# Seven half-size products per pair of columns in the up-projection of a ConvFFN

## The chip, the cores and the metric

One core of one Trainium2 chip runs the kernel. The metric is the device time of one execution in microseconds (us). The kernel before takes 2165.48 us, the median of 3 runs from 2164.55 to 2167.25.

## The reference

The layer mixes tokens in three ways (RWKV-7, latent attention, differential attention), gates and sums the three, projects with w_o and adds the input. Then comes the part that the change is in:

```python
h = RMSNorm(x)                                   # 1024 tokens x 1024
u = h @ w_up                                     # 1024 x 5632: 2816 gate, 2816 val
up = jnp.pad(u, ((0, 0), (CONV_WIDTH - 1, 0), (0, 0)))
u = sum(conv_w[j] * up[:, j:j + S] for j in range(CONV_WIDTH)) + conv_b   # causal, width 3
gate, val = jnp.split(u, 2, axis=-1)
x = x + (jax.nn.silu(gate) * val) @ w_down       # then a final RMSNorm
```

All of it is float32.

## The kernel before, in words

A float32 matmul is made of three: each operand is split into a high part (rounded to the matmul's format) and a low part (the rest), and hi*hi, hi*lo and lo*hi are summed in PSUM. `hilo` makes the parts: ACT copies the high part, POOL or DVE subtracts it for the low part.

`phase_o` takes 8 blocks of 128 tokens: two times 24 matmuls with w_o, DVE adds x out of PSUM, ACT squares and sums, DVE and POOL make the inverse root (`rs_v`, `rs_r`), DVE multiplies (`y`), TensorE transposes y (`ntp`), ACT and DVE write its parts `h2h`, `h2l` (model dimension on the partitions, 8 chunks k of 128; 1024 tokens in the free dimension).

`phase_up` takes the 5632 columns in 44 blocks of 128, gate j and val j alternating (j = 0 to 21). For each block it loads 512 KB of weights, makes their parts (`whi` on ACT, `wlo` on POOL) and runs 2 token halves x 8 chunks x 3 = 48 matmuls of 128x512 into one of two PSUM tiles `ups`. The convolution reads PSUM: ACT writes tap 2 and the bias into SBUF (`cv`), DVE adds the two other taps. ACT takes Silu of the gate, POOL multiplies it with val, and the product `g` stays in SBUF.

`phase_down` does two token groups of 512. In each it goes over 22 blocks j: weights `wdr` from DRAM into parts `wdh`, `wdl` (ACT, DVE), g's parts `gh`, `gl`, and 24 matmuls into 8 accumulators `dps`, one PSUM bank each.

A list scheduler sets the order of each engine's instructions from program order and dependences; every engine then works through its queue in order. All loads and stores here are issued by SP's queue, in order as well. The helpers record the operations, so that in the profile nearly all matmuls are line 65, DVE's and POOL's `tensor_tensor` line 89, `scalar_tensor_tensor` line 99, and ACT's line 86.

## Time and profile before

| | |
|---|---|
| median of 3 runs | 2165.48 us (2164.55 to 2167.25) |
| the profiled execution | 2172.32 us, of which the span is 2170.5 us |
| PE busy | 2098.8 us, 97% |
| DVE, ACT, POOL busy | 945.1, 740.2, 694.0 us |
| output projection | about 1343 to 1438 us |
| up-projection | about 1438 to 1922 us |
| down-projection | about 1913 to 2170 us |
| mean granted clock of TensorE | 0.989 of full speed |

PE, DVE, ACT and POOL are TensorE, VectorE, ScalarE and GpSimd. In a timeline row stand the start, the duration, the engine, the line, the operation, output and inputs with partitions x elements, and in brackets how long the engine was idle before and what released it. A row with "x2" merges two instructions that follow each other; its duration is that of both.

### The profile page before, as it was taken

What the parts mean: (1) busy time and instruction counts of PE and PEld (TensorE: products, weight loads), DVE (VectorE), ACT (ScalarE), POOL (GpSimd) and SP (SyncE); (2) the same over time, 40 slices, a digit from 0 to 9 for tenths busy, and PEclk for the clock granted to TensorE, in tenths of its full rate; (3) what the DMA queues carried; (4) which work ended last, traced back from release to release, by engine and by line L of the source; (5) the groups of instructions that cost most, each with busy time, mean ns of one, the idle gap of its engine ahead of it and who ended that gap; (6) DMA issues with size and microseconds to landing.
All of it is one profiled execution on the core that took longest, in us unless ns stands there. A gap on an engine that the chain in (4) does not pass through costs nothing. (4 is left out here: it accounts for less than half of the span.)

```text
span 2170.5 us, 32037 instructions
## 1 busy us (share of the span) xinstructions
PE 2098.8 (97%) x12818; PEld 1680.4 (77%) x12818; DVE 945.1 (44%) x1956; ACT 740.2 (34%) x1270; POOL 694.0 (32%) x522
## 2 busy tenths in 40 slices
PE   7999999999999998999888999999999999999998
PEld 6877777777777776777677777888888888878887
DVE  7035255243433523566677764432222222243534
ACT  5332222232232223666545442232222222232322
POOL 3152333152243323364155556013333333300000
PEclk9999999999999999999999999999999999999999
DMA  5222232122222214300375444221111111142521
GB/s 178 84 71 78 63 88 66 51 85 62 73 68 78 82 60 131 95 16 11 94 221 175 149 145 160 97 80 49 49 49 49 49 49 49 39 155 98 174 98 59
DMA packets 127447, 191.39 MB, mean 88 GB/s; under 512 B 60064, under 2 KB 64032, under 8 KB 127296
## 3 DMA queue, kind: packets, MB, share of 16 engines
q1 hardware_dynamic: 127296, 189.32, 27.3%
q8 instruction: 101, 1.65, 0.3%
q14 instruction: 50, 0.41, 0.1%
HBM read 147.32 MB, written 41.96 MB: 87 GB/s over the span
## 5 line engine op out<-in xcount | busy, mean ns | idle before, releaser
L89 POOL TENSOR_TENSOR wlo<-wraw,whi 128x512 fp32r<-128x512 f32 (+1 forms) x174 | 276.1, 1594 | 582.4 <-ACT whi L86 245.3
L65 PE MATMUL gps<-hhi,whi 128*128 128x512 f32 (+1 forms) x880 | 346.5, 397 | 8.1 <-ACT sp L86 5.4
L65 PE MATMUL gps<-hlo,whi 128*128 128x512 f32 (+1 forms) x880 | 342.6, 392 | 0.0
L86 ACT ACTIVATE whi<-wraw 128x512 fp32r<-128x512 f32 (+1 forms) x174 | 128.0, 737 | 426.4 <-DMA wraw<-in_w_rest_dram 106.3
L65 PE MATMUL gps<-hhi,wlo 128*128 128x512 f32 (+1 forms) x880 | 226.2, 394 | 2.1 <-DVE lx L99 1.7
L65 PEld LDWEIGHTS gps<-hhi,whi 128*128 128x128 f32 x880 | 168.0, 191 | 49.4 <-ACT sp L86 6.2
L65 PEld LDWEIGHTS gps<-hlo,whi 128*128 128x128 f32 x880 | 167.9, 191 | 36.0 <-issue 4.5
L65 PEld LDWEIGHTS gps<-hhi,wlo 128*128 128x128 f32 x880 | 157.4, 188 | 43.1 <-issue 6.7
L89 POOL TENSOR_TENSOR rs_r<-rs_v,phalf 128x1 f32<-128x1 f32 (+2 forms) x43 | 40.2, 935 | 391.9 <-DVE rs_v L96 383.8
L86 ACT ACTIVATE L<-L,m 128x128 f32<-128x128 f32 (+7 forms) x128 | 98.8, 772 | 69.1 <-DVE m L89 47.5
L77 PE MATMUL ptp<-ident,L 128*128 128x128 f32 x432 | 72.4, 282 | 10.7 <-DVE L L99 2.9
L89 DVE TENSOR_TENSOR gl<-g,gh 128x512 fp32r<-128x512 f32 x43 | 29.5, 692 | 108.8 <-ACT gh L86 107.6
L99 DVE SCALAR_TENSOR_TENSOR st<-pr,gam,fc 128x64 f32<-128x64 f32 x60 | 17.0, 283 | 128.0 <-PE pr L65 127.8
L86 ACT ACTIVATE gh<-g 128x512 fp32r<-128x512 f32 x43 | 26.8, 630 | 131.9 <-PE dps__19477 L65 67.2
L77 PEld LDWEIGHTS ptp<-ident,L 128*128 128x128 f32 x432 | 49.2, 142 | 26.9 <-issue 15.0
L89 POOL TENSOR_TENSOR g<-cv 128x1024 f32<-128x1024 f32 x22 | 52.6, 2390 | 51.7 <-DVE cv L99 50.2
L878 DVE CUSTOM_DVE_ANT_0 L<-S,mband,rq 128x512 f32<-128x512 f32 (+3 forms) x96 | 57.1, 612 | 19.5 <-PE ptp L77 9.7
L89 DVE TENSOR_TENSOR wdl<-wdr,wdh 128x1024 fp32r<-128x1024 f32 x44 | 53.8, 1225 | 15.9 <-ACT wdh L86 15.9
L86 ACT ACTIVATE sp<-gps,hbg 128x512 f32<-128x512 f32 x48 | 32.9, 686 | 75.1 <-PE gps L65 67.9
L65 PE MATMUL bps<-oh,whi 128*128 128x512 f32 x128 | 53.2, 421 | 5.1 <-DVE merged L99 3.2
L89 POOL TENSOR_TENSOR merged<-merged,gth 128x512 f32<-128x512 f32 x32 | 47.6, 1491 | 29.1 <-DVE gth L99 26.3
L878 DVE CUSTOM_DVE_ANT_0 L<-S,bias 128x512 f32<-128x512 f32 (+3 forms) x96 | 50.7, 551 | 12.5 <-PE ptp L77 6.1
(998 smaller groups left out, 4824.3 us busy)
## 6 DMA issues: line engine op xcount, KB each, us to landing
wraw<-in_w_up_dram SPq DMA_DIRECT2D x44, 512.0 KB, 3.3
wdr<-in_w_down_dram SPq DMA_DIRECT2D x44, 512.0 KB, 3.3
wraw<-in_w_rest_dram SPq DMA_DIRECT2D x80, 256.0 KB, 2.9
pD<-sp SPq DMA_DIRECT2D x78, 256.0 KB, 2.0
gth<-pD SPq DMA_DIRECT2D x48, 256.0 KB, 3.0
x<-in_x_dram SPq DMA_DIRECT2D x16, 512.0 KB, 5.5
wraw<-in_w_rw_dram SPq DMA_DIRECT2D x28, 256.0 KB, 3.0
draw<-pD SPq DMA_DIRECT2D x24, 256.0 KB, 5.0
```

Of the source, the lines that this page charges most:

```text
L65: ins = self.nc.tensor.matmul(out, lhsT, rhs, start=start, stop=stop)
L77: self.marked(self.nc.tensor.transpose(out, in_, ident))
L86: self.nc.scalar.activation(out, in_, func, **kw)
L89: (eng or self.nc.vector).tensor_tensor(out, a, b, op)
L99: self.nc.vector.scalar_tensor_tensor(out, a, s, b, op0, op1)
L878: self.nc.vector.tensor_tensor_reduce(L[:, c0:c0 + w], ps[:, :w], bias[:, c0:c0 + w], scale, 3.0e38, ALU.add, ALU.min, acc)
```

## The change

The up-projection of a pair (gate j, val j) is a product of a 2 x 2 block matrix (token halves by halves of the model dimension) with a 2 x 2 block matrix (halves of the model dimension by gate and val). It is now formed by seven products of half the model dimension (12 matmuls each) instead of eight, in the order n2, m4, m3, n5, m1, m6, m7. Each has an operand that is a sum or difference of halves of h, and a weight that is a sum or difference of halves of the two weight blocks:

- The operands of h (`xn2h`, `xm4h`, ... and their low parts) are made in `phase_o` by `operands`, block by block, instead of `h2h` and `h2l`. The halves of blocks 0 to 3 are kept in DRAM (`hD`) and loaded again with blocks 4 to 7; the operands of m6 and m7 go through DRAM as well.
- Per pair DVE makes five weight sums (`wsum`); ACT makes the seven high parts, DVE three low parts (n2, m1, m7) and POOL four. They are made about a pair ahead.
- n2, m3 and m6 are accumulated in PSUM bank b, m4, n5 and m7 in bank c, m1 in bank a. What stands in a bank after each product is read out by ACT (n2, m1) or DVE (the others) into `C` tiles of gate and val, with the sums that the seven products need.
- The convolution reads the `C` tiles. ACT writes tap 2 and bias into a PSUM tile `cvp`, DVE adds the second tap in place there, and the third into SBUF (`cv`). There is one `cvp` tile.
- The product g is stored to DRAM (`gD`) and loaded again by `phase_down` (`down_g`). The weights and g of the first two down blocks are loaded and split during the last pairs, and `down_first` runs their 48 matmuls first.
- From the last block of `phase_o` to the end of `phase_up`, the matmuls are pinned to program order. The products n2 and m4 of pair 0 stand ahead of the last block's transposes.
- Earlier phases: the tiles `merged`, `d0` and `raw` are allocated in token halves, and one load is made in two.

```diff
-    def mm(self, out, lhsT, rhs, start=True, stop=True):
-        ins = self.nc.tensor.matmul(out, lhsT, rhs, start=start, stop=stop)
+    def mm(self, out, lhsT, rhs, start=True, stop=True, **k):
+        ins = self.nc.tensor.matmul(out, lhsT, rhs, start=start, stop=stop, **k)
+        if self.pinned:
+            self.tc.keep_in_program_order(ins)
...
+                if b == 7:
+                    ts = rows()
+                    for m, k in (("n2", 0), ("m4", 4)):
+                        self.up_w[0, m] = self.up_weight(0, m, [t[:, k:k + 4] for t in ts])
+                    self.pinned = True
+                    for m in ("n2", "m4"):
+                        self.up_begin(0, m)
+                    wo.close()
+                    self.up_open(up)
+                    for m in ("n2", "m4"):
+                        self.up_prepare(1, m)
+                y, p = self.norm_rows(x, g, o2, 1), []
...
+    def operands(self, b, p, sp):
...
+        (h0, l0), (h1, l1) = ([t[:, :, bs] for t in self.X[n]] for n in names)
+        self.act(neg, first, scale=-1.0)
+        self.tt(dif, second, neg, ALU.add)
+        self.act(h0, first, scale=-1.0)
+        self.stt(l0, first, -1.0, f32v(h0), ALU.mult, ALU.subtract)
+        self.hilo(h1, l1, dif, lo_eng=vec)
...
+        self.tt(a, a, neg, ALU.add, pool)
+        d = T("xd") if b < 7 else dif
+        self.tt(d, dif, a, ALU.subtract)
+        self.nc.sync.dma_start(kept[2], d)
+        self.tt(c, c, neg, ALU.subtract, pool)
+        self.nc.sync.dma_start(kept[3], c)
+        h, l3, l1 = self.m1(bs)
+        self.act(h, a, scale=-1.0)
+        self.stt(l3, a[:, 0:3], -1.0, f32v(h[:, 0:3]), ALU.mult, ALU.subtract)
+        self.stt(l1, a[:, 3:4], -1.0, f32v(h[:, 3:4]), ALU.mult, ALU.subtract)
...
+            x, y, op = {"n2": ((1, 0), (1, 1), ALU.add), "m4": ((1, 1), None, None), "m3": ((0, 0), None, None),
+                        "n5": ((0, 0), (0, 1), ALU.add), "m1": ((0, 0), (1, 1), ALU.add),
+                        "m6": ((1, 0), (0, 0), ALU.subtract), "m7": ((0, 1), (1, 1), ALU.subtract)}[n]
...
+        vec = w or n in ("n2", "m1", "m7") or j == NFF
...
+        terms = [(k, a, c) for k in range(4) for a, c in ((0, 0), (0, 1))] + [(k, 1, 0) for k in range(4)]
+        for i, (k, a, c) in enumerate(terms):
+            self.mm(ps, w[a][:, k], col(x[c], k), first and i == 0, i == 11, skip_group_check=not first)
...
+            def after(j, n, ps):
+                u, (gate, val) = self.pairs[j], C[j % 2]
+                if n in ("n2", "m1"):
+                    u[n] = T(n)
+                    self.act(u[n], ps)
+                elif n == "m4":
+                    self.tt(val[:, lo], ps, u["n2"], ALU.subtract)
+                elif n == "m3":
+                    u["w"] = T("w")
+                    self.tt(u["w"], ps, val[:, lo], ALU.add)
+                elif n == "n5":
+                    self.stt(gate[:, hi], ps, -1.0, u["w"], ALU.mult, ALU.add)
+                elif n == "m6":
+                    self.tt(val[:, hi], ps, u["m1"], ALU.add)
+                elif n == "m7":
+                    self.tt(gate[:, lo], ps, u["m1"], ALU.add)
+                    conv(j)
...
+                for e in (1, 0):
+                    c, t = j + NFF * e, T("cv%d" % e, S)
+                    x = C[j % 2][e]
+                    ps = cvp.tile([128, S], F32, tag="cv", name="cvp")
+                    self.act(ps, x[:, 2:S + 2], AF.Identity, scale=cw[:, c, 2:3], bias=cw[:, c, 3:4])
+                    self.stt(ps, x[:, 1:S + 1], cw[:, c, 1:2], ps, ALU.mult, ALU.add)
+                    self.stt(t, x[:, 0:S], cw[:, c, 0:1], ps, ALU.mult, ALU.add)
                     ts.append(t)
-                self.act(ts[0], ts[0], AF.Silu)
-                self.tt(self.g[:, j], ts[0], ts[1], ALU.mult, nc.gpsimd)
+                self.act(ts[1], ts[1], AF.Silu)
+                self.tt(ts[1], ts[1], ts[0], ALU.mult, nc.gpsimd)
+                nc.sync.dma_start(self.gD[j], ts[1])
...
+            for j in range(2, NFF):
+                for n in self.ORDER:
+                    after(j, n, self.up_begin(j, n))
+                    self.up_prepare(last[0] + 1, last[1])
+                    last = j, n
+                    if n == "n5":
+                        loads(j + 2)
```

Three places show how the instructions now stand. The first is DVE's queue in the steady up-projection. Before, it held only the two steps of each column's convolution and, once, a low part for the down-projection (`g`):

```order
L99 SCALAR_TENSOR_TENSOR cv<-ups__15996,cw,cv 128x1023 [waits DMAHW0_49,Activation_49]
L99 SCALAR_TENSOR_TENSOR cv<-ups__15996,cw,cv 128x1022 [waits DVE_49]
L99 SCALAR_TENSOR_TENSOR cv<-ups__16055,cw,cv 128x1023 [waits Activation_49]
L99 SCALAR_TENSOR_TENSOR cv<-ups__16055,cw,cv 128x1022 [waits DVE_49]
L89 TENSOR_TENSOR g_18636<-g,g_18636 128x512 [waits DMAHW7_49,Activation_49]
```

Now, from the reading of m6 to that of the next pair's m4 (`C_16166` and `C_16165` are val and gate of one pair, `C_16164` val of the next; `m_` and `n_` are the copies of m1 and n2):

```order
L102 TENSOR_TENSOR C_16166<-ups_b,m_17855 128x512 [waits PE_49,Activation_49]
L102 TENSOR_TENSOR wsum_16087<-wraw 128x512 [waits DMAHW0_49,Pool_49]
L112 SCALAR_TENSOR_TENSOR cvp<-C_16166,cw,cvp 128x1024 [waits Activation_49]
L102 TENSOR_TENSOR C_16165<-ups_c,m_17855 128x512 [waits PE_49]
L102 TENSOR_TENSOR wl<-wsum,wh 128x512 [waits Activation_49]
L112 SCALAR_TENSOR_TENSOR cv_17893<-C_16166,cw,cvp 128x1024 [waits DVE_49]
L102 TENSOR_TENSOR wsum<-wraw 128x512 [waits DVE_49]
L102 TENSOR_TENSOR wl<-wsum_16086,wh 128x512 [waits PE_49,Activation_49]
L102 TENSOR_TENSOR wsum_16086<-wraw 128x512 [waits DVE_49]
L112 SCALAR_TENSOR_TENSOR cvp<-C_16165,cw,cvp 128x1024 [waits Activation_49]
L102 TENSOR_TENSOR C_16164<-ups_c,n_17925 128x512 [waits PE_49]
```

The reading of m4 stands as the eleventh row, ten behind the reading of m6: behind three convolution steps, three sums and two low parts; the fourth step follows it.

The second is DVE's queue at the last block of the output projection. Before, from the block's first addition of x to the low parts of its transposes:

```order
L89 TENSOR_TENSOR x_15880<-ops__15882,x_15880 128x512 [waits DMAHW5_49,DMAHW4_49,PE_49]
L89 TENSOR_TENSOR h2l<-ntp,h2h 128x4x128 [waits Activation_49] x2
L89 TENSOR_TENSOR x_15880<-ops__15908,x_15880 128x512 [waits PE_49]
L96 TENSOR_SCALAR rs_v<-ss 128x1 [waits Activation_49]
L99 SCALAR_TENSOR_TENSOR y<-x_15880,rs_r,gain 128x1024 [waits Pool_49]
L89 TENSOR_TENSOR h2l<-ntp,h2h 128x4x128 [waits Activation_49] x2
```

Now, what stands between the second addition of x and the same block's y (`dif`, `xn5l`, `xm1a`, `xm1b`, `xm3l` and `xd` belong to the block before it, the `wsum` and `wl` to pairs 0 and 1):

```order
L102 TENSOR_TENSOR wsum_16086<-wraw 128x512 [waits DMAHW5_49]
L102 TENSOR_TENSOR wsum_16087<-wraw 128x512
L102 TENSOR_TENSOR dif<-ntp,neg 128x512 [waits Activation_49]
L112 SCALAR_TENSOR_TENSOR xn5l<-ntp,xn5h 128x4x128 [waits Activation_49]
L102 TENSOR_TENSOR wl<-wsum,wh 128x512 [waits DVE_49,Activation_49]
L109 TENSOR_SCALAR rs_v<-ss 128x1 [waits Activation_49]
L102 TENSOR_TENSOR wsum<-wraw 128x512 [waits DMAHW2_49,DVE_49]
L112 SCALAR_TENSOR_TENSOR xm1a<-xa,xm1b 128x3x128 [waits Activation_49]
L112 SCALAR_TENSOR_TENSOR xm1b<-xa,xm1b 128x128
L102 TENSOR_TENSOR wl<-wsum_16087,wh 128x512 [waits Activation_49]
L102 TENSOR_TENSOR xm3l<-dif,xm3h 128x4x128 [waits Activation_49]
L102 TENSOR_TENSOR xd<-dif,xa 128x512 [waits DMAHW4_49]
```

Behind the last of these rows stands y, and on y wait the transposes; on PE they stand behind pair 0's n2 and m4 and ahead of pair 1's n2.

The third is SP's queue at the end of the up-projection. Before, the weights of the down-projection were asked for behind the last load of up weights, and no store of g was there:

```order
L119 DMA wraw<-in_w_up_dram 128x1024 [waits DMAHW1_49,Pool_49]
L1366 DMA gf<-in_norm_final_dram 128x1024 [waits DVE_49,PE_49]
L1354 DMA wdr<-in_w_down_dram 128x1024 [waits PE_49]
L1354 DMA wdr<-in_w_down_dram 128x1024 x2
L1378 DMA x_19330<-xD 128x1024
```

Now, from the loads of g for later blocks (`graw`) over the store of the last pair's g (`gD<-cv_19345`) to the weights of blocks 2 to 5:

```order
L1588 DMA graw<-gD 128x512 [waits DMAHW3_49,DVE_49]
L1546 DMA gD<-cv_19345 128x1024 [waits Pool_49]
L1581 DMA wdr<-in_w_down_dram 128x1024 [waits PE_49]
L1581 DMA wdr<-in_w_down_dram 128x1024 [waits DMAHW2_49,PE_49]
L1581 DMA wdr<-in_w_down_dram 128x1024
L1581 DMA wdr<-in_w_down_dram 128x1024 [waits DMAHW4_49]
L1647 DMA gf<-in_norm_final_dram 128x1024 [waits DMAHW5_49,DMAHW0_49,DVE_49]
```

The four loads stand behind a store that waits for POOL's last product.

## Rows read from the trace of the kernel before

**Rows 1.** The page: span, and busy time of each engine.
```profile
span 2170.5 us, 32037 instructions
PE 2098.8 (97%) x12818; PEld 1680.4 (77%) x12818; DVE 945.1 (44%) x1956; ACT 740.2 (34%) x1270; POOL 694.0 (32%) x522
```

**Rows 2.** Busy time by stretch: start:end, length, then as the first row says.
```profile
core 0: us, PE busy (x) PEld busy (x) DVE busy (x) ACT busy (x) POOL busy (x), PEclk, DMA share, GB/s
1343.00:1438.00 95.00, 94.25 (x441) 77.70 (x440) 40.95 (x60) 24.44 (x43) 7.80 (x9) 1.00 0.23 84
1446.00:1907.00 461.00, 461.00 (x2036) 381.81 (x2035) 109.71 (x87) 121.61 (x109) 153.63 (x64) 1.00 0.14 48
1924.00:1928.00 4.00, 3.78 (x10) 3.02 (x11) 1.49 (x3) 2.51 (x4) 2.37 (x1) 0.58 0.99 348
1928.00:2149.00 221.00, 221.00 (x970) 181.79 (x969) 91.62 (x109) 70.88 (x99) 2.19 (x4) 1.00 0.36 123
```

**Rows 3.** Chain of waits, up-projection: start, us, what.
```profile
1451.06 10.88 PE ups__16055 L65 x48
```

**Rows 4.** Waits of PE from 1340 us on: us in total, times, longest.
```profile
PE ups__15996 L65 <- ACT h2h L86: 0.2, 1, 0.2
PE ups__15996 L65 <- DVE h2l L89: 0.2, 1, 0.2
...
PE dps__18661 L65 <- DVE cv L99: 1.8, 1, 1.8
```

**Rows 5.** Timeline, last block of the output projection, DVE and ACT.
```profile
1438.26 0.69 DVE L89 TENSOR_TENSOR x<-ops__15908,x 128x512 f32<-128x512 f32 x1 [0.83 <-PE ops__15908 L65]
1439.04 1.06 ACT L86 ACTIVATE y<-x 128x1024 f32<-128x1024 f32 x1 [2.43 <-issue]
1441.10 1.28 DVE L99 SCALAR_TENSOR_TENSOR y<-x,rs_r,gain 128x1024 f32<-128x1024 f32 x1 [0.73 <-POOL rs_r L89]
1444.16 1.09 ACT L86 ACTIVATE h2h<-ntp 128x512 fp32r<-128x512 f32 x2 [3.98 <-PE ntp L77]
```

**Rows 6.** Timeline, one column of the up-projection, ACT, DVE and POOL.
```profile
1505.49 1.21 ACT L86 ACTIVATE cv<-ups__16295,cw 128x1024 f32<-128x1024 f32 x1 [0.70 <-PE ups__16295 L65]
1505.59 2.41 POOL L89 TENSOR_TENSOR wlo<-wraw,whi 128x1024 fp32r<-128x1024 f32 x1 [8.48 <-ACT whi L86]
1506.74 2.60 DVE L99 SCALAR_TENSOR_TENSOR cv<-ups__16295,cw,cv 128x1023 f32<-128x1023 f32 x2 [8.28 <-ACT cv L86]
1509.48 2.39 POOL L89 TENSOR_TENSOR g<-cv 128x1024 f32<-128x1024 f32 x1 [1.48 <-DVE cv L99]
```

**Rows 7.** Timeline, DVE and POOL side by side in the attention phase.
```profile
1208.10 1.30 POOL L89 TENSOR_TENSOR wlo<-wraw,whi 128x512 fp32r<-128x512 f32 x1 [0.77 <-ACT whi L86]
1208.39 0.68 DVE L99 SCALAR_TENSOR_TENSOR gth<-gth,bps 128x512 f32<-128x512 f32 x1
1215.42 1.29 POOL L89 TENSOR_TENSOR merged<-merged,gth 128x512 f32<-128x512 f32 x1
1215.51 1.74 DVE L99 SCALAR_TENSOR_TENSOR L<-L,r 128x512 f32<-128x512 f32 x1
```

**Rows 8.** The page's DMA issues: count, KB each, us to landing.
```profile
wdr<-in_w_down_dram SPq DMA_DIRECT2D x44, 512.0 KB, 3.3
pD<-sp SPq DMA_DIRECT2D x78, 256.0 KB, 2.0
```

**Rows 9.** Chain of waits, first matmuls after the last convolution.
```profile
1924.22 1.29 PE dps__18661 L65 x3
1925.51 1.28 PE dps__18662 L65 x3
1926.79 1.28 PE dps__18663 L65 x3
```

**Rows 10.** Timeline, Silu of a gate on ACT.
```profile
1912.05 1.06 ACT L86 ACTIVATE cv<-cv 128x1024 f32<-128x1024 f32 x1 [2.73 <-DVE cv L99]
```

More of the change, by code (lines that the diff above doesn't have):

```diff
@@ L49, in f32v, with __init__, __getitem__ @@
     return ap.bitcast(F32)
+class Halves:
+    def __init__(self, tiles):
+        self.tiles = tiles
+    def __getitem__(self, at):
+        f = at[1].start // 512
+        return self.tiles[f][at[0], at[1].start - 512 * f:at[1].stop - 512 * f]
 class Emit:
@@ new lines, in phase_o, with operand_place @@
+                y, p = self.norm_rows(x, g, o2, 1), []
+                for q in range(2):
+                    p.append(tps.tile([128, 4, 128], F32, tag="ntp", name="ntp"))
+                    for k in range(4):
+                        col = 128 * (4 * q + k)
+                        self.tr(p[q][:, k], y[:, col:col + 128], self.ident)
+                self.operands(b, p, o2)
+                nc.sync.dma_start(self.xD[b], x)
+    def operand_place(self):
+        a = self.mgp.tile([128, 3, 512], F32R, tag="ma0", name="xm1a")
+        b = self.mgp.tile([128, 5, 512], F32R, tag="mb0", name="xm1b")
+        self.X["m1"] = [[b[:, k] for k in range(4)], [a[:, 0], a[:, 1], a[:, 2], b[:, 4]]]
+        self.m1 = lambda bs: (b[:, 0:4, bs], a[:, :, bs], b[:, 4:5, bs])
@@ new lines, in raw_place @@
+    def raw_place(self):
+        a = self.mgp.tile([128, 8, 128], F32, tag="ma1", name="wraw")
+        b = self.mgp.tile([128, 2, 8, 128], F32, tag="mb1", name="wraw")
+        self.raw.update({(1, 1): b[:, 0], (0, 0): b[:, 1], (1, 0): a})
+        for j, e in ((1, 1), (0, 0), (1, 0)):
+            self.up_load(j, e)
+    def operands(self, b, p, sp):
+        lower, vec, pool = b < 4, self.nc.vector, self.nc.gpsimd
+        first, second, names = (p[0], p[1], ("n2", "m4")) if lower else (p[1], p[0], ("n5", "m3"))
+        bs = slice(128 * (b % 4), 128 * (b % 4) + 128)
+        T = lambda tag: sp.tile([128, 4, 128], F32, tag=tag, name=tag, bufs=1)
+        neg, a = T("neg"), T("xa")
+        dif = self.ups.tile([128, 4, 128], F32, tag="b", name="dif") if b < 7 else T("xd")
+        kept = [self.hD[b % 4, k].rearrange("p (k n) -> p k n", k=4) for k in range(4)]
+        if not lower:
+            c = T("xc")
+            self.nc.sync.dma_start(a, kept[0])
+            self.nc.sync.dma_start(c, kept[1])
+        (h0, l0), (h1, l1) = ([t[:, :, bs] for t in self.X[n]] for n in names)
[4 more added lines that the diff above has]
+        self.hilo(h1, l1, dif, lo_eng=vec)
+        if lower:
+            self.act(a, second)
+            self.nc.sync.dma_start(kept[0], neg)
+            self.nc.sync.dma_start(kept[1], a)
+            return
+        self.tt(a, a, neg, ALU.add, pool)
[8 more added lines that the diff above has]
+        self.stt(l1, a[:, 3:4], -1.0, f32v(h[:, 3:4]), ALU.mult, ALU.subtract)
@@ L1314, in phase_up @@
             P = lambda *a, **k: self.pool(es, *a, **k)
[L1315 to L1317 removed]
+            t1 = P("u1", 1)
+            self.upq, cvp = P("upq", 1, space=PSUM), P("cvp", 1, space=PSUM)
+            cw = t1.tile([128, 44, 4], F32, name="cw")
             nc.sync.dma_start(cw, self.i["conv"])
[L1319 to L1324 removed]
@@ new lines, in loads @@
+            def loads(j):
+                for e in (1, 0):
+                    self.up_load(j, e)
+            for m in ("m3", "n5"):
+                self.up_prepare(0, m)
+            for n, m in (("n2", "b"), ("m4", "c")):
+                after(0, n, self.pairs[0][m])
+            start = [((1, "n2"), "0m1"), ((1, "m4"), ""), ((0, "m3"), ""), ((0, "n5"), "1m3 1n5"), ((1, "m3"), "0m6"),
+                     ((1, "n5"), "0m7"), ((0, "m1"), ""), ((0, "m6"), "1m1"), ((0, "m7"), "1m6"), ((1, "m1"), "1m7 2n2"),
+                     ((1, "m6"), "2m4 2m3"), ((1, "m7"), "2n5 2m1 2m6")]
@@ new lines, in phase_up @@
+            for i, (jn, todo) in enumerate(start):
+                after(*jn, self.up_begin(*jn))
+                for t in todo.split():
+                    self.up_prepare(int(t[0]), t[1:])
+                for t, (h, l) in (kept[2 * i - 2:2 * i] if 1 <= i <= 4 else ()):
+                    self.hilo(h, l, t, lo_eng=nc.vector)
+                if jn == (0, "m1"):
+                    loads(2)
+                if jn == (1, "m7"):
+                    loads(3)
+            last = (1, "m7")
+            for j in range(2, NFF):
[5 more added lines that the diff above has]
+                        loads(j + 2)
@@ L1410, in phase_down, with down_accumulators @@
                             for c in range(2):
-                                products(ws, b, c)
+                                self.down_products(ps, ws, b, c)
                         ws = []
+                if not tg:
+                    nc.sync.dma_start(gf, self.i["norm_final"].unsqueeze(0).to_broadcast([128, D]))
                 for b in range(4):
                     finish(tg, b, ws)
+    def down_accumulators(self):
+        return [self.dps.tile([128, 512], F32, tag="d", name="dps_") for _ in range(8)]
     def emit(self):
```

260 lines of the change are left out of this document (161 added, 99 removed).

## The prediction

> **What bounds the kernel now.** I read the page first: TensorE (PE) is busy 97% of the span, every other engine under half [rows 1]. The table by stretch then says where that is strictly so: from 1446 to 1907 us, which is all but the ends of the up-projection, PE is busy 461.00 of 461.00 us at the full clock, 1.00, while VectorE (DVE) does 110, ScalarE (ACT) 122 and GpSimd (POOL) 154 us [rows 2]. The chain of waits runs there over PE alone, one piece for each of 44 columns: 48 matmuls in 10.88 us, so 0.2267 us for one of 128x512 [rows 3]. The waits show no row for PE in that stretch; PE waits at its two ends only, 0.2 + 0.2 us for the last normalised block and 1.8 us for the last convolution [rows 4]. So matmuls taken out of this phase come off the end one for one, until some chain through another engine is longer than PE's new time.
>
> **What is removed.** The code gave the phase 44 columns x 2 token halves x 24 = 2112 matmuls; now 22 pairs x 7 products x 12 = 1848. 264 x 0.2267 = 59.85 us less. A product is 2.72 us, a pair 19.04 us instead of 21.76. The down-projection keeps its 1056 matmuls. Everything else is new work for DVE, ACT, POOL and the queues.
>
> **The steady pair: does DVE keep up?** Price of its pieces: an addition or subtraction of 512 takes 0.69, whether it reads PSUM (x<-ops) or, by half of y's 1024 in 1.28, SBUF [rows 5]; two convolution steps of 1024 take 2.60, so 1.3 each [rows 6]; an ACT pass of 1024 takes 1.21, one of 512 half of 1.09 to 0.6; a POOL low part 1.30 [rows 5 to 7] and the POOL product 2.39 [rows 6]. A pair needs on DVE 5 weight sums, 3 low parts and 5 evacuations (13 x 0.69 = 9.0) and 4 convolution steps (5.2): 14.2 of 19.04 us. ACT has 7 high parts and 2 copies (9 x 0.6) and 3 passes of 1024 (3.5): 8.9. POOL has 4 x 1.30 + 2.39 = 7.6. On the average all fit, so the order decides. Four products (10.88 us) pass between the end of m6 and the start of the next pair's n5, which adds into the bank c that m4 has just filled and must wait until DVE has read m4 out. The order excerpt gives what stands before that read. With m6's end at 0: m6 read out 0.73; weight sum, after POOL's low part (0.04 to 1.34), 2.1; convolution step on val, after ACT's pass (0.77 to 1.98), 3.4; m7 read out 4.0; low part 4.7; second step 6.0; sum 6.7; low part 7.4; sum 8.0; step on gate 9.3; m4 read out 10.0. That is 0.85 us ahead of PE, and m7 (2.72) and the next n2 (5.44) end before DVE comes to them. So I cost the steady state at nothing; the cover is 0.85 us.
>
> No row shows an instruction that writes PSUM from ACT or DVE, as the convolution's first two steps now do. Lower bound: the step that only reads PSUM, 1.3 (a gain below that is not excluded, but is worth nothing while PE does not wait). Upper: the furthest row, a DVE step of 512 that took 1.74 instead of 0.69 [rows 7], 1.05 more on each of two steps: the chain is 12.1, 1.25 us late in each of some 20 pairs, 25 us. I take the lower end, since reading PSUM has cost DVE nothing (0.69 of 512), and keep the other in the range.
>
> **DVE beside POOL.** The rows with 1.74 are the place where it shows: a DVE step with both inputs in SBUF, begun beside POOL's merged<-merged,gth (1.29), took 1.74 us; a DVE step with one input in PSUM beside POOL's wlo took 0.68 [rows 7], and the convolution steps from PSUM took 2.60 beside a POOL low part of 2.41 [rows 6]. So two-SBUF-input steps wait for POOL, by up to 1.05 us, and others do not. In the chain above POOL works from 0.04 to 1.34 (already waited for) and from 8.2 to 9.5, beside the step on gate, which has an operand in PSUM: nothing is added. The Trainium skill (GPSIMD Engine Reference, 1. Specifications) states this as a rule: POOL's SBUF interfaces are shared with VectorE, with contention for DVE instructions with two SBUF inputs; the trace agrees, by those rows. By that rule eight of DVE's seventeen instructions in a pair are exposed, beside five POOL operations, where before the only DVE work beside POOL's three read PSUM.
>
> **The start of the phase.** Before, the last block's y is ready 4.1 us after the output projection's last matmul (1438.26 to 1442.38 [rows 5]), behind nothing, and 24 matmuls (5.44 us) cover it; PE waited 0.48 us [rows 4]. Now 0n2 and 0m4, again 24 matmuls, cover it, but on DVE twelve rows stand between x and y (second excerpt). Counting from that last matmul: x 0.7; two sums, dif, xn5l, wl to 4.0; ACT has five passes before the Square, which ends at 4.0; rs_v 4.2; sum 4.9; xm1a, xm1b behind ACT's xm1b (5.25) to 6.1; wl 6.8; xm3l 7.4; xd 8.0; y 9.3. On POOL xa, xc and two low parts (4 x 1.30) put rs_r at 6.2, earlier than needed. PE is out of work at 5.44: a wait of 3.9 us without the POOL effect. With it, about eight DVE steps there have two SBUF inputs beside four or five POOL operations, and up to 2 of the possible 4 to 5 x 1.05 us end on the path (the rest falls into DVE's waits for ACT): 3.9 to 5.9. Behind it stands a second wait: the copy of 0n2 out of PSUM goes into memory from which xd is stored, so block 7's transposes, neg 0.65, xa 2.0, xm1 3.5, xd 4.1, a store of about 2.0 [rows 8] and the copy put m3 at 7.0, against 5.44 of cover: 1.0 to 1.6. After a PE idle the clock falls: after the 1.8 us idle of before, nine matmuls took 3.85 us instead of 2.04 [rows 9], clock 0.58 over that stretch [rows 2]: 1.8 more. Sum 4.6 + 1.2 + 1.8 = 7.6, less 0.5 of before: **+7** (2 to 13).
>
> **The end of the phase.** Before: 1.84 idle + 1.8 at the half clock = 3.65. Now PE goes from the last m7 (end = T) into 48 matmuls on down blocks 0 and 1, split early, 10.88 us. The accumulators take over the banks that DVE empties last: the second waits for m7's evacuation (T+1.3, 0.6 idle), the seventh for the gate's last convolution step: m6 read out T-2.0, val to T+2.5 (m7 between), ACT 3.75, two steps 6.4, where PE comes at 4.7: 1.7 idle. Then block 2: Silu 1.06 [rows 10] to 7.5, POOL product to 9.9, its store on SP, and only behind it the four loads of down weights (third excerpt), 3.3 us each [rows 8], the first landed at 14.0, its high part 15.1. PE is through blocks 0 and 1 at 13.2 and waits 1.9. Block 2 starts 4.2 late, and 0 to 1.8 of half clock comes on top: 4.2 to 6.0 against 3.65: **+1.5** (0 to 4). g now comes back from DRAM, 256 KB a block beside 512 KB of weights per 5.44 us, some 145 GB/s where the loads alone took 123 on average in that phase [rows 2]; four buffers hide it.
>
> **Sum.** Profiled execution 2172.32 us (span 2170.5, 1.8 outside): 2172.3 - 59.85 + 7 + 1.5 = 2121.0. The median shown, 2165.48, lies 6.84 below the profiled execution, so **2114.1 us**.
>
> **The rivals.** (a) Both ends are hidden after all (DVE's order at the start is slacker than my sum, the banks come free in time): 2165.5 - 59.85 = 2105.6, at most 2108. For it: the output projection leaves DVE room, 41 of 95 us busy [rows 2]. Against it: twelve instructions in order cannot be overtaken. (b) The n5 wait: the PSUM steps cost more, or one or two sums in the chain meet POOL, and 0.85 us of cover is gone. 0.5 to 1.25 us in 20 pairs: 2124 to 2139. Shown by a PE row n5 <- DVE C in every pair. Against: PSUM operands cost nothing so far. (c) Slower: DVE and POOL exclude each other wholly, so that a pair is bound by their sum, 14.2 + 7.6 = 21.8 us, with hand-overs 22.2, instead of 19.04: 3.2 x 20 = +63 against -51: 2177. It decides from 2.6 us a pair on. For it: 1.74 instead of 0.69. Against: only eight DVE steps of a pair have two SBUF inputs, and the convolution beside wlo ran at its usual 2.60 [rows 6]. What the Trainium skill states in the section named gives this rival its condition: with two inputs in SBUF, so not for the rest.
>
> **How the numbers follow.** Likeliest case 68%, its own range 2108 to 2122 (+2 to +13 and 0 to +4 at the ends, not both at an end). (a) 8%. (b) 17%. (c) and other things of that size 7%. To leave out at most 2 in 10, the range takes (a) and most of (b): 2106 to 2137. A measurement here tells 0.2%, 4.3 us, from no change: faster needs under 2161.1, which the first three cases give: 0.92; same only by a (c) of half its size: 0.02; slower 0.06.
>
> **What would show it.** Right: 1848 matmuls at 0.2267 in the phase, no PE wait row between its third pair and its last; PE idle 4 to 6 us at the last transposes with DVE's y as releaser, then about 1 us at m3 behind ACT's n copy; three short idles after the last m7, the last with ACT's wdh after DMA wdr. Wrong: a wait of n5 in each pair (b), DVE instructions on SBUF at 1.7 all through the phase (c), a granted clock under 0.97 between 1470 and 1840, or stretches ahead of the output projection that differ by more than 2 us.

## The result and the profile after

The changed kernel takes 2131.05 us, the median of 4 runs (2127.57 to 2134.91), against 2165.99 us before (4 runs): a ratio of 0.9839, 95% interval 0.9820 to 0.9858. It is faster by 35 us, where 51 were forecast: the time lies in the stated range, 17 us above the value, and outside the 2108 to 2122 us given to the likeliest case. The profiled execution takes 2127.57 us.

The page's span and busy times, which answer [rows 1]:

```profile
span 2125.8 us, 32555 instructions
...
PE 2045.5 (96%) x12554; PEld 1630.5 (77%) x12554; DVE 1148.0 (54%) x2271; ACT 822.6 (39%) x1449; POOL 713.0 (34%) x578
```

There are 264 matmuls fewer, as counted, and PE was busy 53.3 us less instead of 59.85. So part of the shortfall is not waiting. By stretch (columns as in [rows 2]; here the start and the steady part of the up-projection, and the down-projection):

```profile
1434.00:1486.00 52.00, 42.96 (x172) 34.54 (x171) 43.22 (x57) 24.06 (x40) 20.73 (x19) 0.87 0.40 133
1486.00:1880.00 394.00, 392.08 (x1699) 317.79 (x1698) 272.25 (x346) 181.41 (x247) 148.80 (x98) 1.00 0.23 83
...
1896.00:2104.00 208.00, 208.00 (x920) 172.23 (x919) 84.09 (x100) 65.08 (x92) 2.20 (x4) 1.00 0.48 161
```

Where PE stood idle, and for what, from 1330 us on, against [rows 4]:

```profile
PE ntp L90 <- DVE y L112: 7.0, 1, 7.0
PE dps__19364 L76 <- ACT wdh L99: 3.0, 1, 3.0
PE ups_b L76 <- ACT n L99: 2.1, 1, 2.1
PE dps__19370 L76 <- DVE cv L112: 1.4, 1, 1.4
PE dps__19365 L76 <- DVE C L102: 0.5, 1, 0.5
```

Each row is one wait, and each stands where the forecast put one: the last transposes, the copy of n2, and three short ones behind the last m7. Between 1486 and 1860 us there is none. The starts of the matmuls give this account of the two profiled executions, from the first matmul of each stage to that of the next (12 matmuls of the down-projection, which the kernel before ran ahead of its last column, are counted in their own stage):

| stage | before | after | difference |
|---|---|---|---|
| ahead of the output projection | 1342.87 | 1336.30 | -6.57 |
| output projection | 95.19 | 94.52 | -0.67 |
| up-projection | 480.75 | 440.88 | -39.87 |
| down-projection, to its last matmul | 244.33 | 246.57 | +2.24 |
| behind it, with what lies around the span | 9.18 | 9.30 | +0.12 |

The sum is -44.75 us. The first row was not forecast, so the rest gave 38.2 where 51.35 were expected. The difference is in the up-projection: 59.85 us of matmuls went and 39.87 came off the time. 19.98 us were given back there, not 7.

**7.1 of them are in matmuls that take longer.** The chain of waits in the steady part (start, us, what), against 10.88 for 48, or 2.72 for 12, in [rows 3]:

```profile
1498.20 2.72 PE ups_b L76 x12
1500.92 2.72 PE ups_c L76 x12
1503.64 2.80 PE ups_b L76 x12
...
1512.04 2.80 PE ups_c L76 x12
1514.84 2.74 PE ups_a L76 x12
```

These are m6 and m7 of one pair and n2, n5 and m1 of the next. Four of seven products take 2.80 us at a clock of 1.00 and without a wait: their matmuls start every 233.3 ns instead of 226.7. A pair takes 4 x 0.08 + 0.02 = 0.34 us more than 19.04, 7.1 us over 21 pairs.

**The other 12.9 are at the start.** The chain there, from the transposes that wait for y on (0.04 us pieces named issue left out):

```profile
1443.44 1.94 PE ntp L90 x8
1445.38 4.65 PE ups_b L76 x12
1450.03 2.45 PE ups_c L76 x11
1452.48 1.74 DMA cw<-in_conv_dram
...
1454.23 0.61 ACT n L99
...
1454.88 4.43 PE ups_b L76 x12
```

PE waits 7.0 us ahead of the first row and 2.1 ahead of m3 (last row), and after each wait twelve matmuls run largely at the half clock (granted clock 0.57 and 0.65 over them): 4.65 and 4.43 us instead of 2.80, 3.5 us in all. With the transposes' 1.94 that is 14.5; the kernel before lost 1.9 us there in three gaps between its matmuls. The difference is 12.6 of the 12.9. Ahead of `n` the chain names the load of `cw`, which SP issued 0.38 us behind the store of xd; the two land at about the same time, and run 2 tells which of them n waited for.

The queues that make y late, DVE and then POOL (timeline, as in [rows 5]):

```profile
1431.62 3.47 DVE L102 TENSOR_TENSOR wsum<-wraw 128x512 f32<-128x512 f32 x2
...
1436.93 1.63 DVE L102 TENSOR_TENSOR wsum<-wraw 128x512 f32<-128x512 f32 x1
...
1439.15 1.75 DVE L102 TENSOR_TENSOR wl<-wsum,wh 128x512 fp32r<-128x512 f32 x1
...
1442.02 1.27 DVE L112 SCALAR_TENSOR_TENSOR y<-x,rs_r,gain 128x1024 f32<-128x1024 f32 x1
```

```profile
1432.79 1.75 POOL L102 TENSOR_TENSOR xc<-xc,neg 128x512 f32<-128x512 f32 x1
1434.51 3.50 POOL L102 TENSOR_TENSOR wl<-wraw,wh 128x512 fp32r<-128x512 f32 x2
```

Two weight sums take 3.47 us beside POOL where two take 1.28 without it, a third 1.63, a low part 1.75: some 4.2 us over. POOL's own steps stretch from 1.30 to 1.75. y ends at 1443.3, 12.3 us after the last matmul of the output projection instead of 9.3 to 11.3.

**The steady chain** of the forecast is there, DVE's rows from m6's evacuation on:

```profile
1656.06 0.69 DVE L102 TENSOR_TENSOR C<-ups_b,m 128x512 f32<-128x512 f32 x1 [1.28 <-PE ups_b L76]
...
1658.03 1.29 DVE L112 SCALAR_TENSOR_TENSOR cvp<-C,cw,cvp 128x1024 f32<-128x1024 f32 x1
...
1664.75 0.68 DVE L102 TENSOR_TENSOR C<-ups_c,n 128x512 f32<-128x512 f32 x1
```

A step in place in PSUM takes 1.29 us, the lower end. m4 is read out 9.4 us after m6's end, 10.0 in the sum.

**The end** (chain of waits; compare [rows 9] for the half clock):

```profile
1876.81 1.29 DVE cv L112
...
1878.18 1.07 ACT cv L99
...
1879.31 2.40 POOL cv L102
...
1881.73 0.32 SPq L1546
...
1882.10 5.03 DMA wdr<-in_w_down_dram
...
1887.15 1.06 ACT wdh L99
...
1890.02 0.43 PE dps__19370 L76
```

Step, Silu, POOL's product, the store's place in SP's queue, the weights, their high part: each as in the forecast, but the first load of weights took 5.0 us and not 3.3. Behind it some ten matmuls run at the half clock (0.43 us for one).

### The profile page after: what moved, and what is told of

Read it like the earlier page. It is cut to its first block, busy times and chain, and to the rows that moved or that the text cites. A ratio compares the mean times of both kernels' runs of the same rounds, so it can differ in the third digit from the quotient of the medians.

```text
span 2125.8 us, 32555 instructions
## 1 busy us (share of the span) xinstructions
PE 2045.5 (96%) x12554; PEld 1630.5 (77%) x12554; DVE 1148.0 (54%) x2271; ACT 822.6 (39%) x1449; POOL 713.0 (34%) x578
## 5 line engine op out<-in xcount | busy, mean ns | idle before, releaser
L102 POOL TENSOR_TENSOR wlo<-wraw,whi 128x512 fp32r<-128x512 f32 x130 | 169.4, 1313 | 299.2 <-PE gps L76 161.1
L99 ACT ACTIVATE whi<-wraw 128x512 fp32r<-128x512 f32 x130 | 81.3, 628 | 185.0 <-DMA wraw<-in_w_rest_dram 95.2
L99 ACT ACTIVATE wh<-wsum 128x512 fp32r<-128x512 f32 x109 | 68.4, 629 | 135.8 <-PE ups_b L76 60.8
L102 POOL TENSOR_TENSOR wl<-wraw,wh 128x512 fp32r<-128x512 f32 x43 | 57.3, 1334 | 166.1 <-PE ups_c L76 129.3
L102 DVE TENSOR_TENSOR wsum<-wraw 128x512 f32<-128x512 f32 x110 | 81.3, 743 | 41.1 <-POOL wl L102 39.8
L102 DVE TENSOR_TENSOR gl<-graw,gh 128x512 fp32r<-128x512 f32 x42 | 28.9, 692 | 106.3 <-ACT gh L99 106.1
L102 POOL TENSOR_TENSOR wl<-wsum,wh 128x512 fp32r<-128x512 f32 x44 | 57.4, 1304 | 75.0 <-PE ups_b L76 62.1
L99 ACT ACTIVATE gh<-graw 128x512 fp32r<-128x512 f32 x42 | 26.4, 630 | 129.7 <-PE dps__20233 L76 63.6
L90 PEld LDWEIGHTS ptp<-ident,L 128*128 128x128 f32 x432 | 49.0, 141 | 23.9 <-issue 13.2
L102 POOL TENSOR_TENSOR cv<-cv,cv 128x1024 f32<-128x1024 f32 x22 | 53.5, 2434 | 29.6 <-ACT cv L99 29.6
```

The costliest lines, as they stand in the source:

```text
L90: self.marked(self.nc.tensor.transpose(out, in_, ident))
L99: self.nc.scalar.activation(out, in_, func, **kw)
L102: (eng or self.nc.vector).tensor_tensor(out, a, b, op)
```

## The experiments

All times stand against runs of the kernel before on the same chip; the changed kernel's ratio is 0.9839.

**1. y ahead of the put-off work.** Block 6's remaining operand work is recorded behind block 7's y:

```diff
+                y, p = self.norm_rows(x, g, o2, 1), []
+                if b == 7:
+                    for e in (nc.vector, nc.scalar, nc.gpsimd):
+                        self.behind_y.enter_context(tc.issue_after(self.newest(e)))
+                    self.late()
```

> Moved only: the last output-projection block's normalisation (x, rs_v, y) now stands on DVE, ACT and POOL ahead of block 6's late operands, of the weight sums and of the low parts of pairs 0 and 1. Theory (DVE's queue ahead of y, stretched by POOL, is the 7.0 us wait): y ends 4.5 to 5.5 us after the last w_o matmul instead of 12.2, PE waits under 0.5 us at the last transposes instead of 7.0, the half-clock stretch behind it goes too (1.9 + 1.0), so the phase is 9 to 10 us shorter. Rival (the queued work is needed anyway and only moves its wait): PE waits at n2 or m4 of pair 1 or at m3 of pair 0 for block 6's and 7's operands instead, and the phase gets 0 to 3 us shorter.

Measured: 2131.74 us, ratio 0.983 (0.9809 to 0.9851), the same as the changed kernel; in its trace the up-projection is 3.0 us longer (443.84 against 440.88). PE no longer waits for y; it waits for the work put behind it instead:

```profile
PE ups_b L77 <- ACT n L100: 6.6, 1, 6.6
PE ups_b L77 <- DVE xd L103: 5.2, 1, 5.2
```

```profile
1437.02 5.11 DVE L103 TENSOR_TENSOR wsum<-wraw 128x512 f32<-128x512 f32 x3
```

Three sums beside POOL take 5.11 us (second fence, the timeline). The idle moved on. That speaks for the amount of work that DVE has to do beside POOL before PE can go on, and against y's place in it.

**2. The copy of n2 in a place of its own.** The first copy and one C tile are allocated ahead, away from the memory that xd is stored from:

```diff
+            n0 = T("n2")
+            val0 = t1.tile([128, S + 2], F32, name="C01")
...
-                    u[n] = T(n)
+                    u[n] = n0 if (j, n) == (0, "n2") else T(n)
```

> Changed only: the copy of 0n2 and the tile val of pair 0 lie in memory that block 7's kept operands (xa, xc, xd) do not use. Theory (the 2.1 us wait of m3 for ACT's copy n is a wait for the store of xd out of the same memory): the wait goes, and with it part of the half-clock stretch behind it (m3 at 4.43 instead of 2.80): 2 to 4 us less. Rival (m3's own operand, block 7's xm3l on DVE, is as late): the wait stays at 1 to 2 us with DVE as releaser, 0 to 1 us less.

Measured: 2127.59 us, ratio 0.9813 (0.9792 to 0.9834).

```profile
PE ups_c L76 <- DVE C L102: 1.6, 1, 1.6
...
PE ups_b L76 <- ACT n L99: 0.3, 1, 0.3
```

The wait for n falls from 2.1 to 0.3 us, as the theory said: n waited for memory that was being stored, not for the load of `cw`, which it does not read. Others of 1.6 for C and 1.1 for wh come up behind it. Pair 0's m1 starts 34.3 us after the first product instead of 36.9, but 1.9 of these 2.6 us are lost again at the third pair's n5, which is where the wait for C stands. In the trace the up-projection takes 440.12 us instead of 440.88: the mechanism was the theory's, the gain the rival's.

**3. and 4. The weights low in SBUF.** When the products of 2.80 us showed, the first theory was about where in a partition the two operands lie: n2, m4, m3 and n5 have theirs at 18 to 83 KB, and their weights at 168 to 184 KB. One run puts the weights of these four low, the other those of all seven:

```diff
-        w = w or [self.upr.tile([128, 4, 128], F32R, tag=n + m, name="w" + m) for m in "hl"]
+        low = n in ('n2', 'm4', 'm3', 'n5') and (j >= 2 or (n in ("m3", "n5") + self.ORDER[4:])) and self.upl is not None
+        w = w or [(self.upl if low else self.upr).tile([128, 4, 128], F32R, tag=n + m, name="w" + m) for m in "hl"]
...
+                self.upl = self.pool(e4, "upl", 1)
```

> Changed only: the weight parts of n2, m4, m3 and n5 (from pair 2 on for n2 and m4) lie in the low part of the SBUF partition, 89 to 106 KB, near their moving operands at 18 to 83 KB, instead of at 168 to 184 KB. Theory (a matmul takes 233 ns where weights and moving operand lie on opposite sides of the partition, and 227 where they lie on one side): these four products take 2.72 us in the steady pairs instead of 2.80, m1, m6 and m7 stay at 2.72 to 2.74, 20 pairs are 6.5 us shorter. Rival (the first four products of a pair are slow because of what runs beside them, or because of their banks): all seven keep their times, 0 us.

> As the kernel with four weight tiles low, but with all seven low, at 89 to 118 KB; the moving operands of m1, m6 and m7 stay at 152 to 223 KB. Theory of the two sides: n2, m4, m3 and n5 take 2.72 us, and now m6 and m7, and m1 with them, take 2.80: a pair is 0.24 us longer than with four low, 0.08 us shorter than the changed kernel's. Rival (what runs beside, banks): n2 to n5 at 2.80, m6 and m7 at 2.72 as in the changed kernel. A second rival (only the distance from the high end counts, weights low are always fast): all seven at 2.72.

Measured with four: 2123.65 us, ratio 0.9794 (0.9766 to 0.9821), n2 to n5 at 2.72 to 2.73 us. With seven: 2129.6 us (2 runs), ratio 0.9822 (0.9795 to 0.9849); now m6 and m7, whose operands stayed high, are the slower ones:

```profile
1502.64 2.75 PE ups_b L76 x12
1505.39 2.75 PE ups_c L76 x12
```

Both fitted the theory of low and high in kind, though m6 and m7 were expected at 2.80. It was wrong, as runs 9 to 11 show.

**5. The end without SP's queue.** The last product's store goes out on POOL's queue, and the down-projection visits its accumulators in another order, the one that is free last at the end:

```diff
-                nc.sync.dma_start(self.gD[j], ts[1])
+                (nc.gpsimd if j == NFF - 1 else nc.sync).dma_start(self.gD[j], ts[1])
...
+        early = (0, 2, 3, 4, 5, 7, 1)
+        for w, k in [(w, k) for w in ws for k in early] + [(w, 6) for w in ws]:
```

> Changed only at the end of the up-projection: the last pair's g is stored through POOL's own queue instead of SP's, so that SP asks for the down weights of blocks 2 to 5 without waiting for POOL's product; and blocks 0 and 1 visit the accumulator whose bank the last convolution holds (the seventh) last, the one that m7's reading holds (the second) next to last. Theory (the 3.0 us wait at block 2 is the queue on SP, the 0.5 and 1.4 us waits are the banks): all three go, 4.9 us of idle and up to 1.8 us at the half clock: 5 to 6.5 us less from the last m7 to block 3. Rival (block 2 is late because its transfers or the high and low parts behind the last convolution are late anyway): 2 us or more of wait stay at block 2, 2 to 3 us less.

Measured: 2126.31 us, ratio 0.9808 (0.9791 to 0.9824). The wait of 3.0 us for wdh is gone, and the half clock behind it; the down-projection takes 241.7 us instead of 246.6. The waits of 0.5 and 1.4 us stay. The order of visits did change, but the accumulators got their banks in the order of their first use: PE still waits at the second one that it visits (now dps__19366, for DVE's C) and at the seventh (now dps__19365, for DVE's cv). So the gain of 4.9 us is the store's, and another order of banks was not tried.

**6. Only the critical part ahead.** Block 7's y goes first, then the work of block 6 that pairs 0 and 1 need next (`part1`) and the weights of pair 1's m4, then block 7's operands, and the rest of block 6 behind them; with the copy of run 2:

```diff
-                    for m in ("n2", "m4"):
-                        self.up_prepare(1, m)
+                    self.up_prepare(1, "n2")
...
+                if b == 7:
+                    for e in (nc.vector, nc.scalar, nc.gpsimd):
+                        self.behind.enter_context(self.tc.issue_after(self.newest(e)))
+                    self.part1()
+                    self.up_prepare(1, "m4")
```

> At the start of the up-projection, DVE and ACT take what the next products need first: y of block 7, then low parts and xd of block 6 (which free bank b for pair 1's n2), then block 7's n5 and m3 operands; the weight sums of n5, m1 and m6 and the operands of m1 come behind; the copy of 0n2 and val of pair 0 lie in memory of their own. Theory (PE's waits there are DVE's queue with everything in it, of which only a part is urgent, so that order decides): the waits for y (7.0) and xd (5.2 in the run with y first) fall under 1 us each, 0m3 starts 13 to 17 us after the last w_o matmul instead of 23.9, and the phase is 6 to 10 us shorter. Rival (the sum of DVE's work beside POOL in this stretch, some 20 us, bounds PE whatever its order): what is put off is wanted by n5 and m1 of pairs 0 and 1, PE waits there, and 0m6 starts no more than 3 us earlier than in the changed kernel, where it is 39.7 us after the last w_o matmul.

Measured: 2128.35 us, ratio 0.9824 (0.9807 to 0.984), no better than run 2.

```profile
PE ups_b L77 <- ACT n L100: 11.1, 1, 11.1
...
PE ntp L91 <- DVE y L113: 0.4, 1, 0.4
```

y costs 0.4 us, and the work that was put off costs 11.1 in one piece: the chain ahead of n runs over three weight sums on DVE (5.04 us) and two more, over a load of weights that is issued behind them (3.50), to ACT's high part and n behind it in ACT's queue. 0m3 starts 24.1 us after the last w_o matmul and 0m6 40.0 (23.9 and 39.7 in the changed kernel), as the rival said. The same lesson as run 1.

**7. Nothing on POOL at the start.** The sums and low parts of blocks 6 and 7 and of pairs 0 and 1 that POOL made go to DVE:

```diff
-        lower, vec, pool = b < 4, self.nc.vector, self.nc.gpsimd
+        lower, vec, pool = b < 4, self.nc.vector, self.nc.vector if b >= 6 else self.nc.gpsimd
...
-        vec = w or n in ("n2", "m1", "m7") or j == NFF
+        vec = w or n in ("n2", "m1", "m7") or j == NFF or j < 2
```

> Changed only: xa and xc of blocks 6 and 7 and all low parts of the weights of pairs 0 and 1 are made on DVE instead of POOL, so that DVE has 16 rows ahead of block 7's y instead of 12, and POOL has only rs_r. Theory (steps with two inputs in SBUF took 1.6 to 1.75 us there because POOL worked beside them): all of them take 0.7 us or less, and y ends 11 to 12 us after the last w_o matmul although four more instructions stand ahead of it. Rival (POOL is not the reason): the sums stay at 1.6 us, and y ends at 14.5 us or later.

Measured: 2127.43 us (one run); in its trace the up-projection is 1.9 us shorter (438.95). PE waits 5.7 us for y instead of 7.0 although seventeen rows stand ahead of it on DVE instead of twelve (the expectation counted sixteen), and none is stretched:

```profile
1432.99 1.29 DVE L102 TENSOR_TENSOR wsum<-wraw 128x512 f32<-128x512 f32 x2
...
1442.13 1.28 DVE L112 SCALAR_TENSOR_TENSOR y<-x,rs_r,gain 128x1024 f32<-128x1024 f32 x1
```

1.29 for two sums, not 3.47: POOL's steps were what stretched DVE's. The Trainium skill (GPSIMD Engine Reference, 1. Specifications) has POOL's SBUF interfaces shared with VectorE, in contention with DVE instructions of two SBUF inputs; this pair of traces agrees. Here the work on POOL cost DVE more than it saved: with five rows more ahead of it, y ends 11.1 us after the last w_o matmul instead of 12.3.

**8. The gains together.** Runs 2, 3 and 5 in one kernel, with POOL's part of the start as in run 7 (e11) and as in the changed kernel (e12). The store goes out on POOL's queue, as in run 5 (the expectation names ACT's, and calls the up-projection's weights the down-projection's).

```diff
+            n0 = T("n2")
...
+        low = n in ('n2', 'm4', 'm3', 'n5') and ...
...
+                (nc.gpsimd if j == NFF - 1 else nc.sync).dma_start(self.gD[j], ts[1])
```

> All the separate gains in one kernel: n's copy has places of its own, the down-projection's weights lie low in SBUF, wdh's store goes out on ACT's queue with the down-projection's banks in the other order, and POOL makes nothing of pair 0's weights and inputs. Theory (three separate causes that add up): against the changed kernel's 2131.0, n's copy -3.4, the placement -7.4, the end -4.7, POOL taken off 0 to -2: 2113.5 to 2115.5, with every product of a pair at 2.72 to 2.76 us, no wait over 1 us for n, and no 3.0 us wait at the second block of the down-projection. Rival (the gains at the start share one stall: low weights let the operands be written later, since their places lie over tiles of the output projection's last block): the start stays at 13 us over the steady pairs, and the time is 2118 to 2122.

> The same kernel with POOL making its part of pair 0's weights and inputs as in the changed kernel. Theory: 2115.5; if POOL's part of the start decides, 2 us slower than its twin without POOL, with the wait for y at 5 to 7 us; if the queue of DVE decides, within 1 us of it. Rival as for its twin: 2118 to 2122.

Measured: 2116.2 us (5 runs, 2113.5 to 2120.78), ratio 0.9755 (0.974 to 0.977), and 2118.2 us, ratio 0.976 (0.9747 to 0.9773). Both beat both kernels. The runs of before were at 2169.18 in this batch, 3.2 above those beside the changed kernel; by the ratios the gain over the changed kernel is 0.8%, 17 to 18 us, where the expectation summed three gains to 15.5. In the traces the three are 0.8 us (n's copy), 7.9 (low weights, 433.00 us in the up-projection against 440.88) and 4.9 (the store), 13.6 together. e11 has 431.72 us in the up-projection and 241.82 in the down-projection (246.57 in the changed kernel), 13.9 less; e12 432.87 and 241.84, 12.7 less. So in these two stages the gains add up within 1 us; what the ratios show beyond that is open. POOL's part decides nothing by then; the two do not differ. The first waits of e11 (4.9 and 3.3 us in e12):

```profile
PE ntp L90 <- DVE y L112: 4.5, 1, 4.5
PE ups_b L76 <- ACT wh L99: 1.6, 1, 1.6
```

**9. The places by themselves.** A kernel of matmuls alone: five moving operands (ma to me) and five weights (wa to we) at 25 to 205 KB, each with each.

```diff
+            for again in range(2):
+                for w in range(5):
+                    for m in range(5):
+                        for half in range(4):
+                            u = ps.tile([128, 512], F32, tag="u" + "abcde"[w], name="u", bufs=1)
+                            for k in range(12):
+                                self.mm(u, W[w][:, k % 4], M[m][:, k % 4], k == 0, k == 11)
```

> Only matmuls: none of the reference is computed (x is copied to the output, and the sum of one bank is laid over a part of it). Five pairs of tiles, a moving operand m of 4 x 128x512 and weights w of 4 x 128x128, lie at about 25, 76, 127, 174 and 197 KB of each partition (a to e; the weights 8 KB behind their moving operand). Each moving operand is multiplied with each weights, 48 matmuls in a row, all of it twice; nothing else runs beside them. Theory (the pitch hangs on the places of the two operands alone): ma and mb with wd and we 0.233 us for a matmul, md and me with wa and wb 0.229, operands of one neighbourhood 0.2267; mc with wc says where the change lies. Rival (the slower pitch comes from what other engines and transfers write near the weights while PE reads them): all 25 at 0.2267.

Measured: the theory falls. The groups of matmuls (output, inputs, count, then busy us, mean ns, idle us) differ by no more than 1 ns, but for those of ma, the first to write a new bank (in the group of ma with wa, left out here, the run's first product took 4.91 us):

```profile
L76 PE MATMUL u<-me,we 128*128 128x512 f32 x96 | 24.4, 403 | 0.5
...
L76 PE MATMUL u<-mb,wd 128*128 128x512 f32 x96 | 24.4, 403 | 0.5
...
L76 PE MATMUL u<-ma,we 128*128 128x512 f32 x96 | 24.1, 400 | 0.3
```

mb (76 KB) with wd (182 KB) costs what me (197 KB) costs with we beside it, and the first twelve of ma with we, at 25 and 205 KB, take 2.72 us. That all places are alike is also what the rival said, so this run leaves it standing; runs 10 and 11 decide. But the five pairs have one thing in common that the changed kernel's operands have not: every tile begins at a multiple of 128 bytes. By the addresses that the compiler gave, n2 to n5 have operands that begin 32 bytes past a multiple of 128, and weights 96 past one. m6 and m7 have 96 and 96, pair 0's first weights 32 and 32, the kernel before 32 and 32. Run 3 made those of n2 to n5 32 and 32, run 4 made m6 and m7 96 and 32. Of these products, all that ran at 226.7 ns have equal offsets, all that were slower have not (the first few matmuls behind a change of offsets apart).

**10. and 11. 64 bytes.** An unused tile of 64 bytes ahead of the operands makes them 96 like their weights, which stay high; and one ahead of run 3's low weights makes those 96 against 32 again:

```diff
             hp = self.pool(e4, "h2", 1)
+            hp.tile([128, 16], F32, name="pad")
```

```diff
                 self.upl = self.pool(e4, "upl", 1)
+                self.upl.tile([128, 16], F32, name="pad")
```

> An unused tile of 64 bytes ahead of the inputs' operands moves those of n2, m4, m3 and n5 from 32 to 96 bytes past a multiple of 128, as their weights lie (167904 and on are 96 past one); the weights stay at 168 to 184 KB. Theory (a matmul's pitch hangs on whether its moving operand and its weights lie equally past a multiple of 128 bytes): the products of n2, m4, m3 and n5 fall from 2.80 to 2.72 us, the pair from 19.38 to 19.05 to 19.1, the time by 7 to 2124. Rival (what counts is that operands and weights lie in one part of the partition, as the two runs with low weights seemed to say): 2.80 and 2131 as in the changed kernel.

> The kernel with the weights of n2, m4, m3 and n5 low in the partition (beside their operands), and an unused tile of 64 bytes ahead of those weights, so that they lie 96 bytes past a multiple of 128 and their operands 32. Theory (alignment within 128 bytes): 2.80 us for these products and 19.38 for the pair again, the time 2131 as in the changed kernel. Rival (the part of the partition): 2.72 and 2124, as without the 64 bytes.

Measured: 2123.6 us, ratio 0.9807 (0.9785 to 0.983), and 2125.59 us, ratio 0.9816 (0.9794 to 0.9837). The chain of waits in the first (n2 and m1 of one pair):

```profile
1503.47 2.72 PE ups_b L76 x12
...
1514.36 2.72 PE ups_a L76 x12
```

and in the second (n2, m1):

```profile
1500.82 2.80 PE ups_b L76 x12
...
1512.02 2.74 PE ups_a L76 x12
```

The products go with the 64 bytes and not with the part of the partition, in both directions. With them every product takes 2.720 us and a pair 19.04, the forecast's figure; the up-projection takes 433.60 us instead of 440.88. The second kernel's time does not come back to 2131 as expected. Its products did; its up-projection takes 438.53, since the low weights also shorten the start (PE waits 4.9 us for y, not 7.0; why is open). Run 3's gain was thus 5.5 us of alignment (438.53 against 433.00) and some 2 of the start. The rival of run 9 falls as well: in run 10 the same instructions and transfers run beside PE.

The same offsets show in a stage where nobody aimed at them. In the output projection they are 96 and 32, before and after the change; run 10's 64 bytes make them 96 and 96. Its 24 matmuls in the changed kernel, and in run 10:

```profile
1395.35 5.49 PE ops__15790 L76 x24
```

```profile
1396.26 5.45 PE ops__15791 L76 x24
```

That is 229 and 227 ns for one; the stage takes 93.84 us instead of 94.52.

## Why the prediction was right, and where its size was off

- **What is removed:** right in number, 1848 matmuls. The step that failed is the price: 0.2267 us was taken over for all of them, with no term and no rival for a change, and 21 pairs x 48 ran at 0.2333. Forecast 0, measured +7.1, shown by runs 10 and 11.
- **The steady pair:** right. No wait in any steady pair, the chain 9.4 us against 10.0, steps in PSUM 1.29. In six variants (runs 2, 3, 4, 10, 11 and e11 of run 8) PE waits for C once, 1.1 to 2.1 us at the third pair's n5 (1492 us in run 10), and in no pair behind it. There rival (b) has its place right but not its repetition; in the changed kernel none of (a), (b) and (c) happened.
- **DVE beside POOL:** the rule was right, the size too small. "Up to 2" us on y's path were taken; the stretched rows add some 4.2 us on DVE, and y came at 12.3 after the last matmul, 1 us past the end of the range of that step. PE waited 7.0, not 3.9 to 5.9.
- **The start, +7 (2 to 13):** mis-sized term, measured +12.9. Beside y: the wait for the copy of n2 was 2.1, not 1.0 to 1.6 (run 2 shows its cause), and the half clock came after each of the two waits, 3.5 us, where 1.8 was counted once. Two other orders of the same work did not help (runs 1 and 6); run 7 shows that POOL is one reason, 1.9 us in its trace. 4.5 us of the wait for y stay even in e11, where 3.9 were forecast for DVE's queue without POOL.
- **The end, +1.5 (0 to 4):** right, +2.2. Waits of 0.5, 1.4 and 3.0 where 0.6, 1.7 and 1.9 were forecast, and run 5 confirms SP's queue.
- **The sum:** -51.35 was forecast for the profiled execution. 7.1 of slower products, 5.9 of start and 0.7 of end, less 0.7 that the output projection gained, leave 38.3, which is what the three stages gave. The medians differ by 34.9; the 3.3 us between are not explained.
- **Ahead of the output projection** the two executions differ by 6.6 us, which was named as a sign of error. That stretch varies: in the traces of the eleven variants of the changed kernel, which leave its code as it is, its end lies between 1332.95 and 1340.54 us. How much of the 6.6 is the change's tiles in token halves and how much such variation stays open; as the medians differ by less than the three stages gave, they show no gain there.
- **The range:** that it holds owes something to luck. 2131 lies in the band that was given to rival (b), 2124 to 2139, and (b)'s wait is in no pair; the time got there by the slower matmuls and the longer start.

## What to carry to other kernels

Fewer matmuls pay only at the pitch of those that stay: compare the time of equal groups of matmuls in the chain of waits before and after, because a stretch in which PE is 100% busy can still be 3% slow. Where work is put ahead of a stage, count its amount on the engines that PE waits for next: in the two other orders tried here the wait only moved. Work moved from DVE to POOL was no relief at this start, where both had all inputs in SBUF. A wait that is taken away must be followed to the end of the stage: 1.9 of run 2's 2.6 us came back at the next wait. A wait on PE is to be counted with the half clock behind it, for each of the longer ones (2 to 7 us here).

## What the runs showed of the hardware

- The pitch of 128x512 matmuls, each with a new weight load, was 226.7 ns where the moving operand and the weights began equally far past a multiple of 128 bytes in the partition (32 and 32, 96 and 96, and 0 and 0 in run 9's products that begin a new bank), 233.3 ns with 32 and 96, and about 229 with 96 and 32 (m6 and m7 of run 4, the output projection of both kernels). Only these offsets were looked at. Why is open; no engine or transfer was shown to take part.
- Where operands of one residue follow such of another, the first few matmuls are slower too: m1 took 2.76 us in run 3 although both of its operands were at 96, behind n5 at 32, and 2.72 in run 10, where all were at 96.
- In run 9 a product of twelve matmuls into the tile that the one before has just filled took 3.07 us instead of 2.72, the first two 446 and 341 ns after the one before. By the program, its first matmul waits for a semaphore of PE's own last one; whether the bank itself costs anything was not tested.
- DVE steps with two inputs in SBUF, beside POOL: 1.63 and 1.75 us for 128x512 instead of 0.69 (changed kernel), 5.11 for three (run 1). Not each one was stretched: a low part at 1436.22 us in the changed kernel took 0.68, while POOL worked on two of its own. POOL's steps of 128x512 took up to 1.75 us instead of 1.30.
- POOL's rs_r, 128 numbers, took 0.99 us in the changed kernel and 2.06 in run 7, beside such DVE steps. That it waited for DVE there is likely but not shown.
